# Transposes, operand casts and first-stage squares in another order, in a hybrid mLSTM and pooling encoder block

## The chip, the cores and the metric

The kernel runs on one core of a Trainium2 chip, as one launch. The metric is the device time of that launch in microseconds. The core's engines are TensorE (PE, matrix products), VectorE (DVE), ScalarE (ACT), GpSimd (POOL) and SyncE (SP, which here issues nearly all DMAs). Each engine runs its own instructions in program order and waits at semaphores for the others.

## The reference

One encoder layer on x of 2048 tokens by 1024 channels, in float32:

```
h   = rmsnorm(x) modulated by (shift, scale) of c
y   = mixer(h)            # mLSTM on half the channels, pooling on the other half
x   = x + gate * (y @ w_out)
h   = rmsnorm(x) modulated by (shift, scale) of c
x   = x + gate * (relu(h @ w_ff1)**2 @ w_ff2)
out = rmsnorm(x) * g_final
```

The mixer projects h to q, k, v, output gates, scan gates and u; runs a two-directional, chunkwise mLSTM scan over 4 heads; multiplies its normed result by sigmoid(o); and takes centred multi-scale means of u for the rest. The six modulation vectors are silu(c) times a 1024 x 6144 matrix, plus a bias.

## The kernel before

Float32 products are made of three products of parts: a *high* part (a cast to fp32r, on ACT) and a *low* part (the difference, on DVE), as high x high, high x low and low x high.

**The first stage** (0 to 140 us) norms four blocks of 512 tokens and makes v and the gates. For block 0, four loads of x (tiles `xt0` to `xt3`) are squared and summed on ACT (`stats`, L173), POOL makes the reciprocal roots, DVE makes diagonal matrices of them (`dg0`). Then for each of eight channel groups k, DVE makes two modulation sums (`mod_sum`, L117), PE transposes and scales x by the diagonal (`norm_first`, L214, into `xT`), ACT writes the modulated tile (`hf`, L207) and its high part (`Hh`, L208), and DVE the low part (`Hl`, L209). `vg_weights` splits the projection's weights (ACT L228, DVE L229), `vg_mm` does the projection of a 128-token tile. Blocks 1 to 3 (`later_block`) load x in rows (`xs4` and on, three buffers) for the squares `jk4` and on, and transposed (`xk`) for the data; their row statistics reach all partitions through PE (`rms_rows`, L202, `rb`). A scheduler orders this part and the stages up to about 648 us (other projections, the scan), except where `keep_in_program_order` holds an instruction in its place among its engine's instructions.

**The last stage** (from about 648 us) has a hand-written order. Its work is 72 *quads*: 8 of the set Out (y @ w_out, names `o00` to `o13`), 32 of First (h @ w_ff1, `f...`) and 32 of Second (`g...`). A quad handles 256 rows as a 2 x 2 block product in seven products instead of eight (operands 0 to 6: blocks or sums of blocks). A product is 12 matmuls of 128x512 on PE (`product`, L841). `step(t)` emits one step; quad n starts at step 7n, and with d = t - 7n its products stand at d = 0, 2, ... 12, so that from step 6 on each step has one product, taken in turns from two quads. In a step come, in this order: the product and its `post` (DVE add to `acc`, L945, or an ACT copy); for each quad near by its loads, sigmoid (L1004, `SIGM`) and gate (L1010, `GATE`), residual loads, `low_of` (DVE, L779), `sums_of` (DVE, `SUMS`: at d = 0 the two sums `s1`, `s2`, L864 and L865, of which operand 2 is the second), `high_of` (ACT, L776); then pieces of jobs that prepare sums of w_ff2 or h on DVE; then what earlier steps put off. Operand i's high part is made four steps and its low part three steps ahead of its product. There are four buffers for each.

An Out quad's rows, when done, are squared and summed (L953) at d = 13, scaled in place by ACT (`scaled`, L1033, twice) at d = 14, and turned at d = 15 to 18 (`turn`): each turn takes one PSUM bank `t` of two, transposes four 128 x 128 blocks into it (PE, L1043) and copies them with modulation to `hf` (ACT, L1045, in two halves); `put` stores that (L1051), and for the first four quads `sums` makes differences of it that are stored too (L1064). The `ob`, `hf` and job tiles share a pool of five buffers. Out's weights are the parts `ob_0` to `ob_6`, First's `hb`, split as they arrive (ACT L776, DVE L779, 128x1024 each).

## Time and profile before

| | us |
|---|---|
| median of 3 runs | 2110.2 |
| lowest, highest | 2106.39, 2110.89 |
| profiled execution, its own time | 2113.36 |
| its span, first to last instruction | 2111.6 |
| PE busy | 2006.0 |
| DVE busy | 1358.1 |
| ACT busy | 915.9 |

The profiled execution is one of the kernel's executions; its rows are compared with its own 2113.36 us, which is 3.2 us above the median. The stages by time: first stage 0 to 140 us, other projections to 262, scan to 648, Out to about 910, then First and Second to the end. The mean granted clock of TensorE over the span was 0.989 of full speed.

### The profile page before, as it was taken

Reading aid. Unit: us, or ns where it says so; the run is one execution under the profiler, and the core shown is the slowest. Engines: PE = TensorE matmul, PEld = TensorE weight load, DVE = VectorE, ACT = ScalarE, POOL = GpSimd, SP = SyncE. Lnnn points to the kernel's source line nnn. Section 1 sums busy time; section 2 is a strip of 40 time slices with the busy share of each in tenths; the row PEclk is TensorE's granted clock in tenths of the full one; section 3 lists DMA queues with packets and bytes.
Section 4 is the critical chain, followed back from the end, with each engine's and each line's share of the span. In section 5 each row is a group of like instructions: output and inputs, shape, how many; then the busy total and the mean of one; then the engine's idle time right before and its main releaser. Section 6 shows DMA issues by size and latency. Waiting matters only on the chain.

```text
span 2111.6 us, 27742 instructions
## 1 busy us (share of the span) xinstructions
PE 2006.0 (95%) x9591; PEld 1668.3 (79%) x9591; DVE 1358.1 (64%) x2456; ACT 915.9 (43%) x1704; POOL 131.8 (6%) x353
## 2 busy tenths in 40 slices
PE   7999999989999887799999999999999999999998
PEld 6897777878887666578888888888888888888887
DVE  6538646666627555545565766665876867767876
ACT  4631123323326555655555755555522423323432
POOL 1100012212210000100000000000000000000011
PEclk9999999999999999999999999999999999999999
DMA  8736867886548566656666766666887757657554
GB/s 325 231 105 213 274 196 225 253 252 210 177 150 261 175 211 224 198 160 187 197 214 221 232 224 225 208 213 196 289 278 236 264 170 216 245 174 249 202 162 137
DMA packets 298574, 452.87 MB, mean 214 GB/s; under 512 B 23569, under 2 KB 163137, under 8 KB 298306
## 3 DMA queue, kind: packets, MB, share of 16 engines
q1 hardware_dynamic: 228546, 413.35, 60.2%
q10 hardware_dynamic: 69888, 37.76, 5.8%
q8 instruction: 75, 1.23, 0.2%
q14 instruction: 65, 0.53, 0.1%
HBM read 290.40 MB, written 160.62 MB: 214 GB/s over the span
## 4 chain that ended last, share of the span: by engine, by line
PE 81%; DMA 7%; ACT 4%; DVE 4%; issue 2%; SPq 1%; POOL 1%; POOLq 0%; DVEq 0%; ACTq 0%
PE c L404 4%; PE c L405 4%; PE c L403 4%; DMA ua<-uad 2%; DMA ada<-in_w_ada 1%; DMA wotd<-os 1%; DMA vraw<-in_w_v 1%; PE o01x L841 1%; PE g313x L841 1%; PE g312x L841 1%; PE g311x L841 1%; PE g310x L841 1%; PE g303x L841 1%; PE g302x L841 1%; PE g301x L841 1%
## 5 line engine op out<-in xcount | busy, mean ns | idle before, releaser
L403 PE MATMUL c<-Hh,wh 128*128 128x512 f32 x512 | 211.5, 413 | 0.4 <-ACT wh L394 0.4
L404 PE MATMUL c<-Hl,wh 128*128 128x512 f32 x512 | 204.3, 399 | 0.0
L405 PE MATMUL c<-Hh,wl 128*128 128x512 f32 x512 | 203.5, 397 | 0.5 <-DVE wl L395 0.5
L405 PEld LDWEIGHTS c<-Hh,wl 128*128 128x128 f32 x512 | 97.0, 189 | 20.5 <-DVE wl L395 1.0
L403 PEld LDWEIGHTS c<-Hh,wh 128*128 128x128 f32 x512 | 97.2, 190 | 18.3 <-ACT wh L394 1.0
L404 PEld LDWEIGHTS c<-Hl,wh 128*128 128x128 f32 x512 | 97.4, 190 | 16.9 <-issue 0.7
L580 ACT ACTIVATE ua<-ua,vcol 128x128 f32<-128x128 f32 x64 | 25.6, 400 | 104.2 <-POOL ua L576 104.2
L117 DVE SCALAR_TENSOR_TENSOR ada<-ada,c_bc 128x1024 f32<-128x1024 f32 x48 | 58.0, 1220 | 19.1 <-DMA ada<-in_w_ada 19.0
L957 POOL TENSOR_TENSOR g300ss<-g300ss 128x1 f32<-128x1 f32 x2 | 0.9, 452 | 1087.6 <-ACT g300j L953 1087.6
L779 DVE TENSOR_TENSOR wb<-rwb,wb 128x1024 fp32r<-128x1024 f32 x56 | 68.2, 1218 | 0.4 <-ACT wb L776 0.3
L776 ACT CAST wb<-rwb 128x1024 fp32r<-128x1024 f32 x56 | 58.8, 1050 | 11.6 <-DMA rwb<-twd 11.6
L621 ACT ACTIVATE jk<-hm 128x128 bf16<-128x128 f32 x64 | 19.7, 308 | 81.3 <-DVE hm L619 80.7
L585 DVE TENSOR_TENSOR ua<-ua,q 128x256 f32<-128x256 f32 x64 | 26.5, 426 | 35.7 <-DMA ua<-uad 27.4
L576 POOL TENSOR_SCALAR_AFFINE_SELECT ua<-ua 128x128 f32<-128x128 f32 x64 | 24.5, 383 | 271.0 <-DMA ua<-uad 124.7
L624 DVE TENSOR_TENSOR hm<-hm,hss 128x256 f32<-128x256 f32 x32 | 14.8, 462 | 37.4 <-POOL hss L129 37.4
L779 DVE TENSOR_TENSOR ob<-rob,ob 128x1024 fp32r<-128x1024 f32 x14 | 17.0, 1223 | 33.6 <-ACT ob L776 33.3
L255 PE MATMUL vgp<-vgh,Hh 128*128 128x272 f32 x128 | 38.4, 301 | 0.0
L584 DVE TENSOR_TENSOR ua<-ua,S 128x256 f32<-128x256 f32 x64 | 26.5, 414 | 18.2 <-PE S L583 17.4
L256 PE MATMUL v2p<-v2h,Hh 128*128 128x256 f32 x128 | 37.0, 291 | 1.0 <-ACT v2h L236 1.0
L257 PE MATMUL vgp<-vgl,Hh 128*128 128x272 f32 x128 | 37.8, 296 | 0.0
L259 PE MATMUL vgp<-vgh,Hl 128*128 128x272 f32 x128 | 37.4, 294 | 0.0
L258 PE MATMUL v2p<-v2l,Hh 128*128 128x256 f32 x128 | 37.2, 292 | 0.0
(4048 smaller groups left out, 6081.0 us busy)
## 6 DMA issues: line engine op xcount, KB each, us to landing
rwb<-twd SPq DMA_DIRECT2D x56, 512.0 KB, 5.8
ada<-in_w_ada SPq DMA_DIRECT2D x48, 512.0 KB, 5.1
ua<-uad SPq DMA_DIRECT2D x64, 256.0 KB, 3.9
j<-in_w SPq DMA_DIRECT2D x32, 512.0 KB, 5.5
twd<-t SPq DMA_DIRECT2D x64, 256.0 KB, 3.1
twd<-j SPq DMA_DIRECT2D x48, 256.0 KB, 2.7
wr<-in_w_col SPq DMA_DIRECT2D x16, 512.0 KB, 5.2
q<-qkd SPq DMA_DIRECT2D x32, 256.0 KB, 3.6
```

The source lines that it names most:

```text
L117: ve.scalar_tensor_tensor(w, w, 1.0, c_bc, ALU.mult, ALU.mult, accum_out=mod[:, j:j + 1])
L255: pe.matmul(pa[:, :VG], hh, vgh[k], start=st, stop=False)
L256: pe.matmul(pb[:, :256], hh, v2h[k], start=st, stop=False)
L257: pe.matmul(pa[:, :VG], hh, vgl[k], start=False, stop=False)
L258: pe.matmul(pb[:, :256], hh, v2l[k], start=False, stop=False)
L259: pe.matmul(pa[:, :VG], hl, vgh[k], start=False, stop=en)
L403: pe.matmul(ps, hh[:, k], Hh[b][:, k], start=k == 0, stop=False)
L404: pe.matmul(ps, hh[:, k], Hl[b][:, k], start=False, stop=False)
L405: pe.matmul(ps, hl[:, k], Hh[b][:, k], start=False, stop=k == KT - 1)
L776: sc.copy(dst, src)
L779: ve.tensor_tensor(dst, src, asf(hi), ALU.subtract)
L841: pe.matmul(ps, a[:, k], b[:, k], start=start and k == 0 and n == 0, stop=k == 3 and n == 2, skip_group_check=not start)
```

## The change

There are four edits. In `turn`, the four transposes of a bank are issued first and the two copies behind them. Operand 2's high part is made at d = 1 instead of 0, its low part at d = 2 instead of 1 (all 72 quads). In the lead quad (`o00`), the second half's sigmoid and gate come one step earlier (-2 and -1). In the first stage, the small loads `bada` and `gmix` are issued ahead of the four loads of x, the first `vg_weights` stands behind the first `norm_first`, and the squares of block 1 (`jk4` to `jk7`) keep their place in the program, which is behind all of block 0.

```diff
--- before.py
+++ after.py
@@ -134,12 +134,12 @@
 
 
         ts = []
+        bada = small("bada", b_ada, 48)
+        gmix = small("gmix", g_mix, KT)
         for i in range(4):
             t = pv.tile([P, D], F32, tag="xt", name=f"xt{i}", bufs=4)
             dma(t, x[i * P:(i + 1) * P, :])
             ts.append(t)
-        bada = small("bada", b_ada, 48)
-        gmix = small("gmix", g_mix, KT)
         ada = []
         for k in range(0, KT, 2):
             w = big.tile([P, 4, D], F32, tag="big", name=f"ada_{k}")
@@ -171,7 +171,7 @@
             ss = rstd2[:, i:i + 1]
             junk = evt(f"jk{i}").bitcast(BF16)
             ins = sc.activation(junk[:, :D], t, AF.Square, accum_out=ss)
-            if i == 0:
+            if i < 8:
                 tc.keep_in_program_order(ins)
             rstd_of(ss, ss, D)
             return ss
@@ -274,7 +274,6 @@
         for j in range(4):
             ve.tensor_scalar(dg0[:, j], ident, stats(j, ts[j]), None, ALU.mult)
         h_tiles(0)
-        vg_weights(0)
         for k in range(KT):
             mod_sum(8 + k, ada[2 * k])
             mod_sum(k, ada[2 * k + 1])
@@ -282,6 +281,8 @@
             ve.scalar_tensor_tensor(s1[:, k:k + 1], mod[:, 8 + k:9 + k], bsc[:, k:k + 1], gmix[:, k:k + 1],
                                     ALU.add, ALU.mult)
             norm_first(k)
+            if k == 0:
+                vg_weights(0)
             if k % 2 and k < KT - 1:
                 vg_weights(k // 2 + 1)
             if k in (1, 3):
@@ -736,7 +737,10 @@
 
 
 
+
     SUMS = {0: 2, 3: 4, 5: 5}
+    HIGHS = {2 * i - (3 if i == 2 else 4): i for i in range(7)}
+    LOWS = {2 * i - (2 if i == 2 else 3): i for i in range(7)}
     with ExitStack() as fs:
         def room(name, bufs=1, **kw):
             return fs.enter_context(tc.tile_pool(name=name, bufs=bufs, **kw))
@@ -972,8 +976,8 @@
 
                 self.lead = s == j == 0
                 if self.lead:
-                    self.SIGM = {-6: 0, -1: 1}
-                    self.GATE = {-5: 0, 0: 1}
+                    self.SIGM = {-6: 0, -2: 1}
+                    self.GATE = {-5: 0, -1: 1}
                     self.EARLY = {3: (1, 1), 4: (0, 0), 5: (0, 1), 9: (1, 0)}
 
             def post(self, i, ps, slot):
@@ -1038,10 +1042,12 @@
                 hf = self.hf[m] = j4(f"{self.name}hf{m}")
                 for a in range(2):
                     k = 2 * m + a
-                    c = slice(256 * a, 256 * a + 256)
                     for h in range(2):
                         pe.transpose(pt[:, 256 * a + P * h:256 * a + P * h + P],
                                      self.acc[h, k // 4][:, k % 4 * P:k % 4 * P + P], ident)
+                for a in range(2):
+                    k = 2 * m + a
+                    c = slice(256 * a, 256 * a + 256)
                     sc.activation(hf[:, c], pt[:, c], AF.Identity, bias=mod[:, 24 + k:25 + k],
                                   scale=s2[:, k:k + 1])
 
@@ -1165,12 +1171,12 @@
                         (f if callable(f) else getattr(q, f))(when[d])
                 if d in q.EARLY:
                     q.residual(*q.EARLY[d])
-                if (d + 3) % 2 == 0 and 0 <= (d + 3) // 2 < NP:
-                    q.low_of((d + 3) // 2)
+                if d in LOWS:
+                    q.low_of(LOWS[d])
                 if d in SUMS:
                     q.sums_of(SUMS[d])
-                if (d + 4) % 2 == 0 and 0 <= (d + 4) // 2 < NP:
-                    q.high_of((d + 4) // 2)
+                if d in HIGHS:
+                    q.high_of(HIGHS[d])
             if t in jobs:
                 f, *args = jobs[t]
                 active.append(f(*args))
```

Lines behind the edits move: L776 becomes L780, L841 becomes L845, L1033 becomes L1037, L1043 becomes L1046, L1045 becomes L1051.

On PE, the first turn of the third quad (`o02`; `o02t` is the bank, `o02acc` the rows), with the engines that each row waits for. Before:

```order
L841 MATMUL o03x<-ob_6807,o034h 128x512 x2
L841 MATMUL o03x<-ob_6807,o034l 128x512
L1043 MATMUL o02t_7625<-ident,o02acc_7083 128x128 [waits PE_49,Activation_49]
L1043 MATMUL o02t_7625<-ident,o02acc_7417 128x128 [waits Activation_49]
L1043 MATMUL o02t_7625<-ident,o02acc_7083 128x128 [waits Activation_49]
L1043 MATMUL o02t_7625<-ident,o02acc_7417 128x128
L841 MATMUL o10y<-ob_6764,o101h 128x512 x2
```

After:

```order
L845 MATMUL o03x<-ob_6808,o034h 128x512 x2
L845 MATMUL o03x<-ob_6808,o034l 128x512
L1046 MATMUL o02t_7623<-ident,o02acc_7083 128x128 [waits PE_49,Activation_49]
L1046 MATMUL o02t_7623<-ident,o02acc_7415 128x128 [waits Activation_49]
L1046 MATMUL o02t_7623<-ident,o02acc_7083 128x128
L1046 MATMUL o02t_7623<-ident,o02acc_7415 128x128
L845 MATMUL o10y<-ob_6764,o101h 128x512 x2
```

The rows stand in the same order; the third transpose's wait for ACT is gone.

On ACT, the same place, from the cast of operand 5 of the fourth quad (`o035h`) to the second turn's copies (`o102h` is operand 2 of the fifth quad). Before:

```order
L776 CAST o035h_7557<-o03s2_7360 128x512
L953 ACTIVATE o02j10_7568,o02ss1_7433<-o02acc10_7417 128x512
L776 CAST o102h_7593<-o10s2_7590 128x512
L1033 ACTIVATE o02acc10_7417<-o02acc10_7417,o02ss1_7433 128x512
L1033 ACTIVATE o02acc11_7219<-o02acc11_7219,o02ss1_7433 128x512
L776 CAST o036h_7618<-o03y1_7139 128x512
L1004 ACTIVATE o11ob0_7531<-o11ob0_7531 128x512
L1045 ACTIVATE o02hf0_7626<-o02t0_7625,mod_90,s2_92 128x256 x2
L776 CAST o103h_7651<-o10s1_7589 128x512
L1045 ACTIVATE o02hf1_7655<-o02t1_7654,mod_90,s2_92 128x256 x2
```

After:

```order
L780 CAST o035h_7557<-o03s2_7360 128x512
L957 ACTIVATE o02j10_7568,o02ss1_7433<-o02acc10_7415 128x512
L1037 ACTIVATE o02acc10_7415<-o02acc10_7415,o02ss1_7433 128x512
L1037 ACTIVATE o02acc11_7219<-o02acc11_7219,o02ss1_7433 128x512
L780 CAST o036h_7616<-o03y1_7137 128x512
L780 CAST o102h_7620<-o10s2_7590 128x512
L1008 ACTIVATE o11ob0_7531<-o11ob0_7531 128x512
L1051 ACTIVATE o02hf0_7624<-o02t0_7623,mod_90,s2_92 128x256 x2
L780 CAST o103h_7651<-o10s1_7589 128x512
L1051 ACTIVATE o02hf1_7655<-o02t1_7654,mod_90,s2_92 128x256 x2
```

`o102h` moves from ahead of the two scalings to behind them and behind `o036h`; the two copies of a turn stand as before.

On ACT in the first stage, from the end of the fourth channel group of block 0 on (`jk` is a square of block 1, `hf0_k` and `Hh0` block 0's tiles). Before:

```order
L173 ACTIVATE jk4_410,rstd2_94<-xs4_408 128x1024
L207 ACTIVATE hf0_4_360<-xT4_355,mod_90,s1_91 128x512
L208 CAST Hh0_277<-hf0_4_360 128x512
L207 ACTIVATE hf0_5_373<-xT5_368,mod_90,s1_91 128x512
L208 CAST Hh0_277<-hf0_5_373 128x512
L228 CAST vgh3_377<-vraw_217 128x544
L207 ACTIVATE hf0_6_390<-xT6_385,mod_90,s1_91 128x512
L208 CAST Hh0_277<-hf0_6_390 128x512
L173 ACTIVATE jk5_417,rstd2_94<-xs5_415 128x1024
L207 ACTIVATE hf0_7_403<-xT7_398,mod_90,s1_91 128x512
L173 ACTIVATE jk6_424,rstd2_94<-xs6_422 128x1024
L208 CAST Hh0_277<-hf0_7_403 128x512
```

After:

```order
L207 ACTIVATE hf0_4_360<-xT4_355,mod_90,s1_91 128x512
L208 CAST Hh0_277<-hf0_4_360 128x512
L207 ACTIVATE hf0_5_373<-xT5_368,mod_90,s1_91 128x512
L208 CAST Hh0_277<-hf0_5_373 128x512
L228 CAST vgh3_377<-vraw_217 128x544
L207 ACTIVATE hf0_6_390<-xT6_385,mod_90,s1_91 128x512
L208 CAST Hh0_277<-hf0_6_390 128x512
L207 ACTIVATE hf0_7_403<-xT7_398,mod_90,s1_91 128x512
L208 CAST Hh0_277<-hf0_7_403 128x512
L173 ACTIVATE jk4_410,rstd2_94<-xs4_408 128x1024
L173 ACTIVATE jk5_417,rstd2_94<-xs5_415 128x1024
L173 ACTIVATE jk6_424,rstd2_94<-xs6_422 128x1024
```

`jk4` to `jk6` (and `jk7` behind the last row shown) move from between block 0's tiles to behind the last of them. On SP, the load of `xs7` moves behind block 1's four `xk` loads; the rest of the last stage's order on PE and SP is unchanged.

## Rows read from the trace of the kernel before

**Rows 1.** The page, chain of work that ended last, shares of the span by engine.
```profile
PE 81%; DMA 7%; ACT 4%; DVE 4%; issue 2%; SPq 1%; POOL 1%; POOLq 0%; DVEq 0%; ACTq 0%
```

**Rows 2.** Busy time by stretch: length, PE, PEld, DVE, ACT, POOL (instructions), PE clock, DMA, GB/s.
```profile
658.20:909.88 251.68, 203.20 (x885) 159.73 (x886) 144.49 (x229) 142.33 (x269) 20.69 (x48) 0.96 0.65 203
...
1200.00:2111.00 911.00, 904.00 (x3989) 748.20 (x3987) 647.26 (x953) 376.45 (x628) 18.77 (x48) 1.00 0.66 218
```

**Rows 3.** PE's waits, 690 to 912 us: total us, times, longest; best and worst quad.
```profile
PE o12t L1043 <- ACT o12hf L1045: 7.9, 4, 2.4
...
PE o00t L1043 <- ACT o00hf L1045: 3.9, 4, 1.8
PE o12t L1043 <- ACT o12acc L1033: 1.4, 1, 1.4
...
PE o13t L1043 <- ACT o13acc L1033: 0.8, 1, 0.8
```

**Rows 4.** Timeline of PE, a steady turn: start, length, instruction, [idle before, releaser].
```profile
729.79 0.38 PE L1043 MATMUL o01t<-ident,o01acc 128*128 128x128 f32 x2
730.89 0.44 PE L1043 MATMUL o01t<-ident,o01acc 128*128 128x128 f32 x2 [0.72 <-ACT o01hf L1045]
731.09 0.71 PE L841 MATMUL o03x<-ob,o032h 128*128 128x512 f32 x2
...
733.95 0.38 PE L1043 MATMUL o01t<-ident,o01acc 128*128 128x128 f32 x2
```

**Rows 5.** Timeline of PE, second pair of transposes in quad o02's first turn.
```profile
749.83 0.44 PE L1043 MATMUL o02t<-ident,o02acc 128*128 128x128 f32 x2 [1.78 <-ACT o02hf L1045]
```

**Rows 6.** Timeline of ACT ahead of that turn.
```profile
746.43 0.62 ACT L776 CAST o102h<-o10s 128x512 fp32r<-128x512 f32 x1 [4.41 <-PE o03x L841]
746.96 1.33 ACT L1033 ACTIVATE o02acc<-o02acc,o02ss 128x512 f32<-128x512 f32 x2
```

**Rows 7.** Timeline of DVE ahead of that cast.
```profile
745.65 0.69 DVE L865 TENSOR_TENSOR o10s<-o10s,o10y 128x512 f32<-128x512 f32 x1
```

**Rows 8.** Timeline of PE, the starts of two plain products in the last stage.
```profile
1551.68 0.61 PE L841 MATMUL g002z<-wb,g0025h 128*128 128x512 f32 x2
...
1554.40 0.61 PE L841 MATMUL g003x<-wb,g0032h 128*128 128x512 f32 x2
```

**Rows 9.** Timeline of DVE there, the low of the quad ahead's last operand.
```profile
1553.05 0.68 DVE L779 TENSOR_TENSOR g0026l<-g002w,g0026h 128x512 fp32r<-128x512 f32 x1
```

**Rows 10.** Busy time by stretch, a middle quad and a late quad of Out.
```profile
789.93:817.13 27.20, 22.04 (x102) 17.27 (x101) 15.54 (x29) 14.32 (x29) 2.49 (x6) 1.00 0.76 235
...
875.52:905.03 29.51, 23.63 (x101) 18.41 (x101) 15.33 (x21) 19.78 (x34) 3.51 (x6) 0.94 0.48 152
```

**Rows 11.** Timeline of PE, the lead quad's third product and the next one.
```profile
658.20 1.22 PE L841 MATMUL o00x<-ob,o002h 128*128 128x512 f32 x2 [4.88 <-ACT o002h L776]
...
663.20 0.63 PE L841 MATMUL o00z<-ob,o003h 128*128 128x512 f32 x2
```

**Rows 12.** Timeline of ACT there: the lead quad's second sigmoid and third operand.
```profile
654.09 0.62 ACT L1004 ACTIVATE o00ob<-o00ob 128x512 f32<-128x512 f32 x1
...
657.53 0.62 ACT L776 CAST o002h<-o00s 128x512 fp32r<-128x512 f32 x1 [2.34 <-DVE o00s L865]
```

**Rows 13.** Timeline of DVE there: the second low of part ob_4.
```profile
654.22 1.23 DVE L779 TENSOR_TENSOR ob<-rob,ob 128x1024 fp32r<-128x1024 f32 x1 [0.17 <-ACT ob L776]
```

**Rows 14.** Timeline of ACT in the first stage: the square of xs4.
```profile
37.03 1.06 ACT L173 ACTIVATE jk<-xs 128x1024 bf16<-128x1024 f32 x1 [5.54 <-DMA xs<-in_x]
```

**Rows 15.** Timeline of PE in the first stage, block 0's scaled transposes.
```profile
38.89 1.44 PE L214 MATMUL xT<-dg,xt 128*128 128x128 f32 x5 [5.30 <-ACT hf L207]
```

**Rows 16.** Busy time by stretch, right after that wait.
```profile
40.00:45.00 5.00, 5.00 (x25) 5.00 (x25) 5.00 (x12) 2.71 (x4) 0.00 (x0) 0.50 0.40 164
```

**Rows 17.** Timeline of DVE in the first stage, the low of block 0's fifth part.
```profile
39.52 0.69 DVE L209 TENSOR_TENSOR Hl<-hf,Hh 128x512 fp32r<-128x512 f32 x1 [3.92 <-ACT Hh L208]
```

**Rows 18.** PE's waits from 0 to 140 us, those for the statistics of blocks 1 to 3.
```profile
PE rb L202 <- DVE dg L190: 4.6, 3, 2.1
```

## The prediction

> **What bounds the kernel now.** I read the chain of waits first, then the busy time by stage, then PE's waits in the one stage that stands out, then single instructions there. The chain is 81% PE [rows 1]: only PE time, or a wait of PE, can be won. By stage [rows 2], from 1200 us to the end PE is busy 904.00 of 911.00 us, so nothing is to be had there but something can be lost. In the Out stage, 658.20 to 909.88 us, PE is busy 203.20 of 251.68 us: 48.5 us idle at a mean granted clock of 0.96, with neither ACT (142.33) nor DVE (144.49) full. PE's waits tell where [rows 3]: eight quads have four turns each, and in each quad the transposes wait four times for the copy `hf`, 3.9 us a quad in the best one and 7.9 in the worst (the eight sum to 39.2 us); once in each quad the first transposes also wait for `acc`, the scaling on ACT, 0.8 to 1.4 us (9.4 us in all). 39.2 + 9.4 = 48.6 is the whole idle time.
>
> A steady turn [rows 4]: first pair of transposes at 729.79, then a wait of 0.72 us for ACT's copy of that first pair, second pair at 730.89, product at 731.09, next turn at 733.95. Two transposes take 0.20 us with nothing in between (730.89 to 731.09); so the turn took 1.30 us, where four transposes need 0.40. In a quad's first turn the wait for the copy is 1.78 us [rows 5], because ACT reaches the copy late. Why it is late stands in [rows 6, 7]: on ACT `o102h` starts at 746.43, and only then the two scalings (746.96, 1.33 us); the profile names a product as what `o102h` waited for, but the sum it reads (`o10s`, L865) ran on DVE from 745.65 to 746.34, which fits its start to 0.1 us. So the third operand's cast holds the scaling, the scaling holds the first transposes, and the casts behind it hold the first copy.
>
> **The change, part by part.** *Turns.* With four transposes first and the copies behind, the third transpose has no wait. A turn is then 4 x 0.10 = 0.40 us, plus 0.14 us by which the product behind a turn is longer (2.86 from 731.09 to 733.95, against 2.72 between the starts of two plain ones [rows 8]): 0.54. The copies start 0.2 us later on ACT, which nothing on PE needs before the bank's next turn but one; that costs nothing while ACT has room, and 0.2 us a turn if it has none.
>
> *Third operand a step later.* The cast now stands behind the two scalings and `o036h`. Scaling then needs only the quad's row statistics, which do not depend on that sum, so it leaves the path: the 9.4 us of `acc` waits and the surplus of the first `hf` waits go. What comes late next is the third operand itself. Its low part is now made one product after its old place: after a product, DVE does the post add, the low of operand 6 and then this low, 3 x 0.68 = 2.0 us [rows 9]. The next product but one needs it with its third matmul, 2.72 + 2/12 x 2.72 = 3.17 us after the same end: 1.1 us spare. Where a job's sums are on DVE too, `g0026l` starts at 1553.05 [rows 9], so this low would end 2 x 0.68 later, at 1554.4, and is needed 0.45 us behind 1554.40 [rows 8]: 0.4 us spare. I take 0 us for all 72 quads; the bounds are 0 and, in a few quads with both a job and a new weight part on DVE (one more 0.68 in the way), 0.3 us.
>
> *The Out stage summed.* From 658.20 to 909.88 lie 63 products and 32 turns: 63 x 2.72 + 32 x 0.54 = 171.4 + 17.3 = 188.7 us against 251.7, 63.0 us less. That holds 48.5 of idle time and 14.5 of PE time that was longer than 2.72 a product: short stops stretch the matmuls behind them, and after the long ones the granted clock was lower (0.94 over the quad at 875.52 [rows 10]; the product at 658.20 took 5.0 us to 663.20, its first pair 1.22 us, the next product's 0.63 [rows 11]). Per quad this is 7 x 2.72 + 4 x 0.54 = 21.2 us instead of 27.2 [rows 10].
>
> *The lead quad.* PE waits 4.88 us for `o002h` [rows 11]. On ACT [rows 12] the sigmoid at 654.09 comes behind two casts of `ob_4`, which wait for their DMA; DVE then needs gate, sum and sum, and `o002h` runs at 657.53. Now sigmoid, gate and sums stand before those casts. But `o002h` still queues behind the casts and the copy L986: the copy takes the sigmoid's slot at 654.1, and if it is as long as that (0.6) `o002h` ends at 655.3. On DVE its low stands behind `ob_4`'s second low, which starts at 654.22 and ends at 655.45 [rows 13], and an add: 656.0 to 656.7, a 1 us wait inside the product. Effective start 656.3 instead of 658.20: 1.9 us. `o001h` now stands behind that sigmoid and a copy, up to 1.2 us later, under the product ahead of its own: 0, with 1.2 us lost as the bound. Out: 63.0 + 1.9 = 64.9.
>
> *What remains in Out.* In the last quads ACT is busy 19.78 us in 29.51 [rows 10] and would have 21.2; transposes or products will wait for it here and there. 1 to 2 us in each of the last three quads, up to 0.5 in each of the others: 6 us taken (bounds 0, and 18, 6 us for each of the three, as if the whole difference of their PE period, 27.2 to 21.2, stayed). Out: 59 us.
>
> *First stage.* ACT's square of `xs4` stands ahead of `hf0_4` and waits 5.54 us for its load [rows 14]; PE waits 5.30 us behind it [rows 15], and then runs 5 us at a granted clock of 0.50, the lower of the two levels (1.2 GHz), after the stop [rows 16]. With the squares behind block 0, `hf0_4` goes as soon as its scale is ready. DVE, which waited 3.92 us to 39.52 for what comes of it [rows 17], then goes on at 35.6: 3.9 us. The clock loss is 5 x 0.5 = 2.5 us. Against it, block 1's squares now run together behind `Hh0_7`, and the fourth one's load waits for the first square's buffer; PE's waits for these statistics were 4.6 us in three blocks [rows 18] and may grow or shrink, since the same change puts PE's `rb` matmuls behind more projection work. Bounds: nothing (the late squares take it all back) and 5.3 + 2.5 + 4.6 = 12. I take 7, the two measured parts 3.9 + 2.5 and half a us. The stages between are PE's own and pass it on.
>
> *`bada` and `gmix` ahead of `x`.* Two SP issues, 0.95 us; the first squares come that much later, the modulation's first sum that much earlier. 0, with 1.5 us lost as the bound. On small transfers, the Trainium skill ("DMA: Bandwidth & Descriptors", section "Why small descriptors are slow (HBM only)") speaks against it, with 27% overhead for 256-byte pieces; worked out from that page for the 28 KB here it is an estimate of 0.1 us, below what the sum takes. No row of this case shows these two loads ahead of `x`.
>
> **Sum.** 59 + 7 = 66 us from the profiled execution's 2113.4: 2047. That execution was 3.2 us above the median of 2110.2, so on the median 2044.
>
> **Rivals.** (1) *Transfers become the bound in Out.* In a middle quad the DMA engines are busy 0.76 of 27.20 us [rows 10], 20.7 us, and the new period is 21.2: 98%. Loads of `y` and stores of `hf` share few buffers, so full queues would hold the gate or the copy. For it: that share. Against: only the four quads of the first half store the extra differences, and loads are issued nine steps ahead. If no more than 85% can be had, such a quad takes 24.3 us: 3.1 us x 4 = 12 lost, 2056. The Trainium skill (the same page, "Where 436 GB/s comes from") gives 435 GB/s at most; by that page a quad's 6.4 MB are an estimate of 14.7 us, and this rival would be void. The trace does not agree: 235 GB/s at a share of 0.76 [rows 10] are 309 GB/s while busy, and I go by that row. (2) *The first turn keeps its wait*: if the scaling waits for something else than the cast, 9.4 + 8 x 1.1 = 18 us stay: 2062. With no gain in the first stage added to either, 2067 to 2069. (3) *The change does not do what it says in the turns*, the copies being needed before the fourth transpose: then only the third operand, the lead quad and the first stage help, about 20 us: 2090. (4) *Slower: the third operand's low comes too late on DVE.* It decides from its spare time of 0.4 to 1.1 us; to outweigh 66 us over the 64 quads behind Out, each must wait more than 1.03 us, so the low must come 1.4 to 2.1 us later than worked out in every quad. At 1.3 us a quad: 83 us lost, 2127. DVE, busy 647.26 of 911.00 us [rows 2], speaks against it.
>
> **How the numbers follow.** Forecast (gain of 54 to 82, 2028 to 2056): 0.70. Rivals 1 and 2, or no gain in the first stage on top of some residue, 2056 to 2068: 0.16; worse mixtures of these to 2085: 0.06. Rival 3: 0.03. Rival 4: 0.03, and 0.02 that some of it cancels the gain. Range 2028 to 2068. A measurement of this kernel tells 0.2% (4.2 us) from no change: faster 0.95, same 0.02, slower 0.03.
>
> **What would show it.** Right: no wait of a transpose for `hf`, none or nearly none for `acc`; a quad period near 21.2 us in the middle of Out; Out's 63 products and 32 turns in 188 to 206 us; `xT` of block 0 without a wait of 5 us; plain products still 2.72 us apart from 1200 us on. Wrong: PE waiting for lows of operand 2 in the First or Second quads; PE waiting in Out for casts that wait on loads, with the DMA share near 1; projection matmuls of blocks 1 to 3 waiting longer for their statistics than 4.6 us.

## The result and the profile after

The changed kernel takes 2054.86 us (median of 4 runs, 2052.05 to 2058.01) against 2110.51 for the kernel before (4 runs): a ratio of 0.9741, 95% interval 0.9722 to 0.9760, or 55.7 us. The time lies in the stated range (2028 to 2068), 11 us above the forecast of 2044. The profiled execution took 2054.10 us, 59.3 less than the profiled one of before; the steps below are compared between these two.

The page of the profile after, busy time, and the chain that ended last (it answers to [rows 1]):

```profile
PE 1991.4 (97%) x9591; PEld 1659.4 (81%) x9591; DVE 1356.0 (66%) x2456; ACT 917.9 (45%) x1704; POOL 132.0 (6%) x353
...
PE 74%; DMA 7%; DVE 4%; ACT 1%; issue 1%; SPq 1%; POOL 1%; POOLq 0%; DVEq 0%; ACTq 0%
```

PE is busy 14.6 us less than before (2006.0) with the same 9591 instructions. Most of that is the granted clock: in the trace of before, PE is busy for 35.2 us in stretches at 0.50, the lower of the two levels (1.2 GHz), and after for 12.6 us; at half speed the difference is worth 11.3 us.

Busy time by stretch, after, with the columns of [rows 2]. The first stretch answers to the Out stage there, from the effective start of the lead quad's third product to the same product of the First set as before; the second to the end of the kernel:

```profile
649.06:850.42 201.36, 192.36 (x884) 157.06 (x884) 142.45 (x227) 139.18 (x266) 23.01 (x48) 0.97 0.81 254
...
1143.40:2050.00 906.60, 901.26 (x3977) 746.18 (x3975) 645.26 (x952) 378.15 (x624) 18.70 (x48) 1.00 0.66 217
```

Out fell from 251.68 to 201.36 us; its idle PE time from 48.5 to 9.0. Behind Out nothing moved: the first product of quad `f010` starts 59.34 us earlier than before (893.94 against 953.28), and the last matmul of the kernel again 59.34 us earlier.

PE's waits in Out after (as [rows 3]):

```profile
PE o13t L1046 <- ACT o13acc L1037: 3.2, 1, 3.2
PE o12t L1046 <- ACT o12acc L1037: 2.8, 1, 2.8
PE o01t L1046 <- ACT o01acc L1037: 0.5, 1, 0.5
PE o02t L1046 <- ACT o02acc L1037: 0.4, 1, 0.4
PE o03t L1046 <- ACT o03acc L1037: 0.4, 1, 0.4
PE o10t L1046 <- ACT o10acc L1037: 0.2, 1, 0.2
```

All 32 waits for `hf` are gone. What is left of the turns' waits are those for the scaling, 7.5 us in sum, 6.0 of it in the last two quads. In the second of these waits, and 1.2 us behind the end of the first (811.65), the granted clock falls to the lower level, for 6.8 and 3.4 us (busy time by stretch, columns of [rows 2]):

```profile
812.87:816.29 3.42, 3.42 (x10) 2.58 (x9) 0.00 (x0) 2.28 (x5) 0.00 (x0) 0.50 0.95 323
836.77:843.59 6.82, 5.98 (x16) 4.72 (x17) 1.08 (x1) 3.63 (x7) 0.03 (x1) 0.50 0.14 40
```

PE is busy for 9.4 us there, which costs about 4.7 us.

Timeline of PE, a turn of quad o02 after (it answers to [rows 4]):

```profile
726.77 0.39 PE L845 MATMUL o10y<-ob,o101l 128*128 128x512 f32 x1
727.00 0.60 PE L1046 MATMUL o02t<-ident,o02acc 128*128 128x128 f32 x4
727.36 0.71 PE L845 MATMUL o03z<-ob,o035h 128*128 128x512 f32 x2
...
730.20 0.60 PE L1046 MATMUL o02t<-ident,o02acc 128*128 128x128 f32 x4
```

Four transposes stand in one row and take 0.36 us to the next product; from turn to turn 3.20 us, where it was 4.16.

But the first turn of most quads still waits. Timeline of ACT around it, quad o02 (it answers to [rows 6, 7]):

```profile
723.08 1.33 ACT L1037 ACTIVATE o02acc<-o02acc,o02ss 128x512 f32<-128x512 f32 x2 [4.10 <-DMA xad<-o02acc]
724.33 0.60 ACT L780 CAST o036h<-o03y 128x512 fp32r<-128x512 f32 x1
724.83 0.61 ACT L780 CAST o102h<-o10s 128x512 fp32r<-128x512 f32 x1
```

And of SP, which issues the DMAs:

```profile
717.05 2.74 SPq L1070 DMA_DIRECT2D thd<-o01T  x4
719.88 0.42 SPq L1186 DMA_DIRECT2D xad<-o02acc  x1
```

`o102h` is behind the scaling, as the change wants it. The scaling now waits 4.10 us for something else: it overwrites `o02acc` in place, and the store of the unscaled row to `xad`, which reads `o02acc`, must be through. SP issued that store only at 719.88, behind four stores of the last quad's sums.

### The profile page after: what moved, and what is told of

It reads as the page before. It is cut to its first block, busy times and chain, and to the rows that moved or that the text cites. A ratio compares the mean times of both kernels' runs of the same rounds, so it can differ in the third digit from the quotient of the medians.

```text
span 2052.2 us, 27784 instructions
## 1 busy us (share of the span) xinstructions
PE 1991.4 (97%) x9591; PEld 1659.4 (81%) x9591; DVE 1356.0 (66%) x2456; ACT 917.9 (45%) x1704; POOL 132.0 (6%) x353
## 4 chain that ended last, share of the span: by engine, by line
PE 74%; DMA 7%; DVE 4%; ACT 1%; issue 1%; SPq 1%; POOL 1%; POOLq 0%; DVEq 0%; ACTq 0%
PE c L406 3%; PE c L405 3%; PE c L404 3%; DMA ua<-uad 2%; DMA ada<-in_w_ada 1%; DMA os<-in_w_o 1%; PE g313x L845 1%; PE g312x L845 1%; PE g311x L845 1%; PE g310x L845 1%; PE g303x L845 1%; PE g302x L845 1%; PE g301x L845 1%; PE g300x L845 1%; PE g213x L845 1%
## 5 line engine op out<-in xcount | busy, mean ns | idle before, releaser
L581 ACT ACTIVATE ua<-ua,vcol 128x128 f32<-128x128 f32 x64 | 25.7, 401 | 106.8 <-POOL ua L577 106.8
L780 ACT CAST wb<-rwb 128x1024 fp32r<-128x1024 f32 x56 | 58.7, 1050 | 24.9 <-DMA rwb<-twd 24.8
L625 DVE TENSOR_TENSOR hm<-hm,hss 128x256 f32<-128x256 f32 x32 | 14.6, 457 | 39.0 <-POOL hss L129 39.0
L440 ACT COPY u<-c 128x512 f32<-128x512 f32 x16 | 9.4, 586 | 62.6 <-PE c L406 62.6
L585 DVE TENSOR_TENSOR ua<-ua,S 128x256 f32<-128x256 f32 x64 | 26.5, 414 | 14.6 <-PE S L584 14.2
```

The costliest lines, as they stand in the source:

```text
L585: ve.tensor_tensor(W, W, S[:, 0:P].unsqueeze(1).broadcast_to([P, 2, P]), ALU.mult)
L780: sc.copy(dst, src)
```

## Experiments: the parts alone

Each of the first four kernels is the kernel before with some of the change's edits. All medians of these four are compared with 2110.75 us, the kernel before on the same chip (19 runs).

**Turns alone.** Of the change only this:

```diff
                 for a in range(2):
                     k = 2 * m + a
-                    c = slice(256 * a, 256 * a + 256)
                     for h in range(2):
                         pe.transpose(...)
+                for a in range(2):
+                    k = 2 * m + a
+                    c = slice(256 * a, 256 * a + 256)
                     sc.activation(hf[:, c], pt[:, c], ...)
```

> Only the order inside a turn is changed: four transposes, then two copies. Theory (the wait for the copy is the turns' own, the wait for the scaling is the third operand's): the 39.2 us of waits for hf go, the 9.4 us for acc stay or grow a little, and part of the 14.5 us of stretched matmuls goes: 42 to 50 us less than before, about 2064. Rival (the transposes then wait for the scaling for longer, since ACT is late in every first turn): acc waits of 2 us and more a quad, 30 to 38 us less, about 2076.

Measured: 2063.35 us, ratio 0.9772 (0.9755 to 0.9788), 47.4 us less. PE's waits there:

```profile
PE o13t L1042 <- ACT o13acc L1033: 3.1, 1, 3.1
PE o12t L1042 <- ACT o12acc L1033: 2.3, 1, 2.3
PE o03t L1042 <- ACT o03acc L1033: 1.2, 1, 1.2
```

Five more quads wait 1.2 us each as o03 does. So the copy's wait was the order of the turn, and the waits for the scaling stayed at 1.2 us, as the first theory had it; in o12 and o13 they grew from 1.4 and 0.8 to 2.3 and 3.1. That PE now comes there earlier fits this, but was not tried by itself.

**Third operand alone.**

```diff
+    HIGHS = {2 * i - (3 if i == 2 else 4): i for i in range(7)}
+    LOWS = {2 * i - (2 if i == 2 else 3): i for i in range(7)}
...
-                if (d + 3) % 2 == 0 and 0 <= (d + 3) // 2 < NP:
-                    q.low_of((d + 3) // 2)
+                if d in LOWS:
+                    q.low_of(LOWS[d])
```

(and the same for `high_of` with `HIGHS`)

> Only operand 2's high and low part are a step later. Theory: the acc waits (9.4 us) go, and each first turn's wait for hf falls from 1.8 to the 0.7 of the other turns (8 x 1.1 us): 12 to 18 us less than before, about 2095; from 1200 us on products stay 2.72 us apart. Rival (the cast was not what held the scaling): no change, 2108 to 2112. Second rival (the later low is too late on DVE): slower than before, with PE waiting for lows of operand 2.

Measured: 2106.69 us (10 runs, 2099.79 to 2110.39), ratio 0.9977 (0.9965 to 0.9990): 4.1 us less, a third of what was expected. Its profiled execution (2102.33) is the second fastest of the ten. There six of eight waits for `acc` are gone, but the wait for the first copy hardly fell. Four rows of PE's waits there:

```profile
PE o02t L1045 <- ACT o02hf L1047: 3.9, 4, 1.7
...
PE o00t L1045 <- ACT o00hf L1047: 3.6, 4, 1.5
PE o12t L1045 <- ACT o12acc L1035: 1.3, 1, 1.3
PE o13t L1045 <- ACT o13acc L1035: 0.8, 1, 0.8
```

The longest wait for a copy is 1.5 to 1.8 us in the first five quads, where 0.7 was expected: the casts between the scaling and the first copy still stand there, `o102h` itself among them. The mechanism for `acc` is confirmed, the second term was wrong. And ACT already waits for something new here, which costs PE nothing in this quad yet (the first turns of o02 and o03 are still 25.7 us apart):

```profile
ACT o02acc L1035 <- DMA xad<-o02acc: 2.9, 1, 2.9
```

**Both.**

> Turns and third operand together, first stage and lead quad as before. Theory (the rest of the change is worth 5.8 us in the first stage and 3.3 in the lead quad): 45 to 50 us less than before, about 2064. If the two parts only overlap, it is no faster than the better of the two alone; if each takes its own wait, it is 10 to 16 us faster than the turns alone.

Measured: 2057.98 us, ratio 0.9748 (0.9728 to 0.9769), 52.8 us less: 5.4 us better than the turns alone, half of the least that was expected (the intervals of the two overlap), and again 2.4 and 2.8 us of waiting for `acc` in o12 and o13.

**The first stage alone** (small loads first, `vg_weights(0)` behind `norm_first(0)`, squares of block 1 kept in program order; the edits as in the change):

> Only the first stage's edits (small loads first, weights split later, squares behind block 0). Theory: 5 to 6.5 us less than before, all of it there by the last projection of v and kept to the end, about 2104.5. Rival (the gain is lost again in the scheduled stages behind): under 2 us.

Measured: 2107.11 us (10 runs), ratio 0.9980 (0.9970 to 0.9989), 3.6 us less, between theory and rival. In its profiled execution the last projection of v is 6.5 us earlier than in that of before, but 4.5 us of that are lost again in Out, with the same waits as before. What differs there is the granted clock; busy time by stretch of about one quad, in that execution:

```profile
740.00:767.00 27.00, 21.84 (x100) 17.13 (x99) 15.34 (x29) 14.32 (x29) 2.49 (x6) 1.00 0.72 219
767.00:797.00 30.00, 24.91 (x103) 19.30 (x101) 15.85 (x29) 14.42 (x29) 2.48 (x6) 0.89 0.65 195
797.00:825.00 28.00, 22.85 (x99) 17.96 (x98) 12.11 (x20) 14.32 (x29) 1.92 (x6) 0.94 0.68 217
```

Per matmul that is 0.218 us at a clock of 1.00 and 0.242 at 0.89, so the second stretch has 2.4 us more PE time for its 103 matmuls. That execution (2111.49) is the slowest of this kernel's ten, so its loss is not the rule; the median counts.

**The change without one part.** Three single executions, to be read by places and not by totals.

Without the small loads first:

```diff
-        bada = small("bada", b_ada, 48)
-        gmix = small("gmix", g_mix, KT)
         for i in range(4):
             ...
+        bada = small("bada", b_ada, 48)
+        gmix = small("gmix", g_mix, KT)
```

> The whole change without the small loads ahead of x. Theory (the two issues cost the start 0.7 us): the first transposed matmul is at 11.7 us instead of 12.4, the last v projection up to 1 us earlier, the total the same within its interval. Rival (the modulation sums wait for bada): the start moves, but the first scale of block 0 does not, and nothing is gained behind it.

The first transposed matmul is at 11.76 us against 12.38: these loads ahead of x cost 0.6 us there, and this is clear of the spread (11.6 to 11.8 in all five executions without them, 12.3 to 13.5 in all nine with them). The last v projection is 0.9 us earlier (132.92), which is inside the spread of that place. The total (2051.26) is within the spread of the change's runs.

With the squares where they were (`if i == 0:` in `stats`):

> The whole change, with the squares of the second block where the scheduler put them before. Theory (the first stage's gain is theirs): PE waits some 5 us again behind the square of xs4, and the last v projection is back at 136.5 to 140.5 us instead of 133.8. Rival (the later split of the weights makes the gain): it stays at 133 to 135.

Timeline of PE in the first stage there (2057.05 in all):

```profile
39.92 2.08 PE L214 MATMUL xT<-dg,xt 128*128 128x128 f32 x8 [5.47 <-ACT hf L207]
```

The wait of 5.30 us [rows 15] is back as 5.47, and the last v projection is at 140.47 us. The first stage's gain is the squares': with the small loads first and the weights split later, but without them, nothing is won.

Without the earlier sigmoid and gate (`SIGM` -1 and `GATE` 0 again):

> The whole change without the earlier sigmoid and gate of the lead quad. Theory (they are worth the difference between 4.9 and 1.5 us of waiting at that quad's third product, and a shorter time at the lower clock): the gap from its second to its third product is 6.9 to 7.8 us instead of 3.7, and what follows runs as in the whole change.

Timeline of PE at the lead quad's third product there (2059.47 in all):

```profile
657.84 1.22 PE L844 MATMUL o00x<-ob,o002h 128*128 128x512 f32 x2 [5.72 <-ACT o002h L779]
```

The gap from the lead quad's second to its third product is 8.60 us (649.24 to 657.84) instead of 3.70, a little more than expected. The seven executions with both this edit and the later third operand show 3.70 to 4.75.

## Experiments: what holds the last quads

The waits in o12 and o13, and the scaling's wait for the store, were left. Each kernel here is the whole change with one more edit. They ran on several chips, on which the kernel before took 2110.47 to 2112.71 us; a difference between the medians of two of them is uncertain by about as much, 2 us.

**Squares first.** Work that a step has put off is done in the order in which it was put off; here the square of a finished row is taken ahead.

```diff
-            for f, args in later.pop(t, ()):
+            for f, args in sorted(later.pop(t, ()), key=lambda e: getattr(e[0], "__name__", "") != "square"):
```

> The whole change, and of the work that a step has put off the sum of squares of a finished row is done first, ahead of the casts of the next set's weight parts and of the turns' copies (other work of a step keeps its order). Theory (the 2.8 and 3.2 us for which PE waits for acc in quads o12 and o13 come from ACT, where the square stands behind those casts, so that POOL's root comes late and ACT then waits for it): both waits fall to under 1.5 us, the granted clock in these quads stays nearer 1.00, and the time falls by 4 to 7 us against the whole change, to about 2049. Rival (ACT is simply full there): the waits stay near 6 us in sum, 2052 to 2057.

Measured: 2050.99 us, ratio to before 0.9714 (0.9698 to 0.9731). By the medians that is 3.9 us less than the change, but the two intervals overlap, so the gain is not clear of the spread. Nor did it come as expected: o12 still waits 2.5 us and o13 2.2. In this execution the granted clock in the last quads stayed at 1.00, where the change's fell for 3.4 and 6.8 us; but it also stayed there in the run without the earlier sigmoid, whose squares stand as in the change. ACT's waits name the other cause:

```profile
ACT o02acc L1036 <- DMA xad<-o02acc: 4.0, 1, 4.0
...
ACT o12acc L1036 <- DMA xad<-o12acc: 3.7, 2, 1.9
```

**No scaling in place.** DVE makes a diagonal of the reciprocal roots, the turns multiply by it, nothing overwrites the row.

```diff
             def scaled(self, h):
-                for a in (self.acc[h, 0], self.acc[h, 1]):
-                    sc.mul(a, a, self.ss[h][:, 0:1])
+                self.dg[h] = pdg.tile([P, P], F32, tag="dg", name=f"{self.name}dg{h}")
+                ve.tensor_scalar(self.dg[h], ident, self.ss[h][:, 0:1], None, ALU.mult)
...
-                        pe.transpose(pt[...], self.acc[h, k // 4][...], ident)
+                        pe.matmul(pt[...], self.acc[h, k // 4][...], self.dg[h],
+                                  start=True, stop=True)
```

> The whole change, but Out's rows are no longer scaled in place by ACT: DVE makes a diagonal matrix of the reciprocal roots, and the turns multiply by that instead of transposing with the identity (as the first stage does). Theory (after the change ACT waits 2 to 4 us in each quad for the store of the unscaled row, which reads what the scaling overwrites, and PE's waits for acc in o01 to o10 and in o12 come of that): ACT has no wait for that store, PE's waits for acc or the diagonal fall from 7.4 us in sum to under 3 us, and the time falls by 3 to 7 us against the whole change, to about 2050. Rival (the waits in o12 and o13 are a full ACT or a late root): o12 and o13 still wait 4 us or more in sum for the diagonal, 2053 to 2057. Third: if a product with the diagonal takes longer on PE than a transpose, 128 of them show it in the time of a turn.

Measured: 2056.88 us, ratio 0.9748 (0.9733 to 0.9762), no gain. Yet the waits fell as the theory has it, to 1.1 us in o12 and 0.5 in o13, with none in the six quads ahead of them; so a late root alone does not explain them. The third possibility took the gain; timeline of PE, a turn:

```profile
730.39 1.05 PE L1046 MATMUL o02t<-o02dg,o02acc 128*128 128x128 f32 x8
731.20 0.71 PE L845 MATMUL o03z<-ob,o035h 128*128 128x512 f32 x2
```

Four products with the diagonal run as eight matmuls and take 0.81 us to the next product, where four transposes took 0.36: 32 turns x 0.45 = 14.4 us more. With squares first on top:

> The diagonal of the run before it, and the squares of finished rows first among the work put off. Theory (store and late root are two causes): o12 and o13 wait under 1 us in sum, 6 to 10 us less than the whole change, about 2047. If the diagonal alone already takes all waits, the two runs agree within 1 us.

2055.39 us, ratio 0.9743 (0.9726 to 0.9760): o12 and o13 wait 0.5 us each, and the total stays, for the same reason.

**Stores first.** Scaling in place again; in the list of work put off, the stores and the squares of finished rows come first, so that SP issues the store ahead of the loads of weight parts, which wait for their buffers, and of the stores of `hf` and of its sums.

```diff
-            for f, args in later.pop(t, ()):
+            for f, args in sorted(later.pop(t, ()), key=lambda e: not (
+                    e[0] is dma or getattr(e[0], "__name__", "") == "square")):
```

> The whole change with scaling in place; of the work put off in a step, the stores of finished rows and their squares come first, so that on SP the store no longer stands behind the loads of the next set's weight parts, which wait for their buffers. Theory (the store is late because it is issued late): ACT's waits for it fall from about 4 to 2 us in o01 to o10, little in PE's time there, and o12's wait falls by 1 us or more: 4 to 7 us less than the whole change, as with squares first or a little more. Rival (the store is late because transfers are slow, a DMA share of 0.85 to 0.96 in these quads): the waits stay as they are.

Measured: 2040.90 us (2038.86 to 2043.78), ratio to before 0.9675 (0.9656 to 0.9694): 70.8 us less than before, 14 less than the change and 10 less than squares first. It beats both kernels. Out, from the lead quad's third product to the first of `f010`, takes 232.6 us in the profiled execution, against 245.6 in that of the change and 240.2 with squares first: 13.0 and 7.6 us of the gains are there, and the rest lies ahead of that, where the kernels are the same. (The edit also takes stores in Second ahead; from `f010` on, both the change and this version take 1150.7 to 1150.8 us.) PE's waits for `acc`, all that there are:

```profile
PE o13t L1045 <- ACT o13acc L1036: 1.0, 1, 1.0
```

ACT's waits for the store, the two that are left:

```profile
ACT o02acc L1036 <- DMA xad<-o02acc: 2.1, 1, 2.1
ACT o10acc L1036 <- DMA xad<-o10acc: 1.8, 1, 1.8
```

Around the same place as above, the timeline of SP:

```profile
712.15 0.49 SPq L1186 DMA_DIRECT2D xad<-o02acc  x1
712.73 1.04 SPq L1056 DMA_DIRECT2D h2d<-o01hf  x2
713.83 2.36 SPq L1069 DMA_DIRECT2D thd<-o01T  x4
```

and of ACT:

```profile
716.49 1.34 ACT L1036 ACTIVATE o02acc<-o02acc,o02ss 128x512 f32<-128x512 f32 x2 [2.06 <-DMA xad<-o02acc]
```

The store goes ahead of 3.4 us of other issues, and the scaling is through at 717.8, 0.9 us ahead of the turn's first transpose (718.66). In the change it was through at 724.4, 1.2 us behind the turn's first transpose (723.21). From o02 to o13 quads are 20.96 us apart. Transfers were not short: in this kernel's busiest stretch the DMA share was 0.99 and PE waited for nothing:

```profile
788.00:809.00 21.00, 21.00 (x102) 17.38 (x101) 18.61 (x24) 19.91 (x36) 4.23 (x6) 1.00 0.99 311
```

**Stores first, without the later third operand.**

> The version with stores and squares of finished rows first, without the later third operand (all other parts of the change kept). Theory (the cast of the third operand held the scaling as worked out, and its gain was hidden because the store then held it): PE waits about 1.2 us for acc in each of seven or eight quads again, 8 to 10 us in sum instead of 1.0, and the time is 8 to 12 us above the 2040.9 us of the version with it, about 2050. Rival (with the store early, the cast no longer matters, since the scaling is reached in time either way): the waits stay near 1 us in sum, 2039 to 2043.

Measured: 2053.01 us, ratio 0.9719 (0.9695 to 0.9742), 12.1 us above the version with it. Two rows of PE's waits:

```profile
PE o12t L1043 <- ACT o12acc L1034: 1.3, 1, 1.3
PE o03t L1043 <- ACT o03acc L1034: 1.2, 1, 1.2
```

Seven quads wait 1.2 or 1.3 us for `acc` again and o13 1.0: 9.5 us in sum. So by the medians the later third operand is worth 12 us where the store is in time, and 5.4 where it is not (turns alone against both). In the profiled executions the waits for `acc` fall by 8.6 us (9.6 to 1.0) and by 5.9 (12.6 to 6.7), and Out by 11.0 (243.6 to 232.6) and by 3.2 (246.6 to 243.5). So the late store and square hold back some 3 us of waiting. The rest of the difference is in good part the clock: with both, it fell to the lower level for 6.8 us right at the wait in o13, and neither with the turns alone nor in these two versions did it fall in the last quads. Busy time by stretch, both:

```profile
838.20:845.00 6.80, 6.06 (x17) 4.80 (x18) 0.99 (x2) 3.68 (x7) 0.00 (x0) 0.50 0.14 39
```

## Why the prediction was right, and where it was not

The time came out inside the range, and most of the gain (47.4 of 55.7 us) comes from the mechanism that was forecast for the turns. By the medians the gain is near the lower end of the forecast one (54 to 82). Term by term, by the two profiled executions:

| term | forecast | measured |
|---|---|---|
| Out, steady part | 57.0 | 251.68 - 201.36 = 50.3 |
| lead quad | 1.9 | 3.3 |
| first stage | 7 | 5.8 |
| stages between, First, Second | 0 | 0 |
| sum | 66 | 59.3 |

**Turns: right.** No wait for `hf` is left, a turn has one row of four transposes, and turns alone gave 47.4 us. From turn to turn 3.20 us pass, 0.48 more than a product's 2.72, where 0.54 was forecast.

**Third operand: the wrong step is "scaling then needs only the quad's row statistics".** It also needs the store of the row that it overwrites. In the trace of before nothing waits for that store, because the cast held the scaling for longer than the store did; the step should have asked which other reader of `acc` is late when the cast is gone. This is the prediction's second rival, come true in part: the scaling does wait for something else, but PE's waits for `acc` are 7.5 us, 6.0 of them in two quads, and not 9.4 with another 8.8 for the first copies. The runs show it from three sides: ACT waits 2.9 us for `xad` with the third operand alone and 4 us in the change; making the store earlier takes PE's waits for `acc` from 6.1 us with squares first to 1.0, and 7.6 us off Out; and the third operand takes 8.6 us of these waits away then, 5.9 before. The term "the surplus of the first `hf` waits" did not come from this part either; the turns' order takes it.

**What remains in Out: 6 us forecast, 12.7 measured** (201.36 against the ideal 188.7). Of that 9.0 is idle PE time (7.5 for `acc`, 0.9 for the low of `o012`, the rest in small pieces) and 3.7 more busy time: the two stretches at the lower clock cost about 4.7, and the cheaper turns give 1.9 back. The sum had no term for the clock here. The place was right, the last quads, but the cause was put down to a full ACT; it was the store and the late square, for with both first, ACT is busy 19.91 of 21.00 us in such a stretch and PE waits for nothing. Of the two the store is the one that is shown, since squares first left 4.7 us of waiting in o12 and o13.

**Lead quad: 3.3 instead of 1.9, in part luck.** PE waits 0.81 us for `o002h` and 0.73 for its low (1 was forecast). As forecast, `o002h` stands behind two casts of `ob_4`; but these started 2.95 us behind the quad's first product (641.91), as their load landed, where before it was 4.02 (651.74 against 647.72). Timeline of ACT after:

```profile
644.86 1.05 ACT L780 CAST ob<-rob 128x1024 fp32r<-128x1024 f32 x1 [1.11 <-DMA rob<-wotd]
```

In the other six executions with both the earlier sigmoid and the later third operand they started 3.3 to 4.0 us behind it, and the lead quad gained 2.3 to 3.0 us against before. Timeline of PE after:

```profile
648.33 0.73 PE L845 MATMUL o00x<-ob,o002h 128*128 128x512 f32 x2 [0.81 <-ACT o002h L780]
649.79 0.50 PE L845 MATMUL o00x<-ob,o002l 128*128 128x512 f32 x1 [0.73 <-DVE o002l L783]
```

Here, with a shorter stop, the first pair took 0.73 us instead of 1.22 [rows 11], and the granted clock stayed at 1.00.

**First stage: mis-sized.** The pair of profiled executions shows 5.8 us, but the last v projection varies without the change (136.6 to 139.6 in the four executions whose first stage is as before) and with it (132.7 to 137.4 in eight): 138.0 and 134.6 on the mean, 3.4 us. The stage alone gave 3.6 by its median. With the change the spread is the granted clock again: 132.7 to 134.1 in the five executions where it stayed at 1.00 between 60 and 140 us, 135.8 in the two where it fell for 3.4 us near 95 us, and 137.4 in the one where it fell for 6.8 us, at a wait of PE for a block's statistics (stores first without the later third operand, busy time by stretch):

```profile
94.50:101.20 6.70, 5.88 (x27) 5.89 (x28) 5.34 (x10) 3.89 (x6) 0.65 (x3) 0.50 0.41 120
```

DVE's 3.9 us were there (the low of `hf0_4` starts at 36.58 instead of 39.52, and `hf0_2` had been 1.0 us later than before), and so was what the prediction set against them without taking any of it off: the fourth square comes last and waits for its load. Timeline of ACT after:

```profile
50.49 1.06 ACT L173 ACTIVATE jk<-xs 128x1024 bf16<-128x1024 f32 x1 [1.54 <-DMA xs<-in_x]
```

The diagonals of block 1 are complete at 52.9 us (53.9 before): block 1 goes on only 1 us earlier. PE's waits for such statistics did not grow, though: 3.5 us in sum instead of 4.6 [rows 18].

**The small loads** cost 0.6 us at the first matmul, inside the bound of 1.5; taken as 0.

**Rivals.** Transfers did not become the bound: the share rose, to 0.79 to 0.89 over the change's quads and to 0.98 over one of stores first, and no wait of PE in Out names a load. At a share of 0.99 the engines moved 311 GB/s, as the 309 worked out from [rows 10] had it. That one store held the scaling was a matter of where it stood in SP's order. The rival of a late low came true once outside the lead quad, 0.88 us in o01, more than the 0.3 us that was its bound for a quad; there Out's weight parts and the lead quad's extra adds are on DVE. A load has a part in it: DVE waited 1.33 us for a residual and then ran without a stop up to this low. Timelines of DVE and PE after:

```profile
660.50 0.69 DVE L949 TENSOR_TENSOR o01acc<-o01x,o01acc 128x512 f32<-128x512 f32 x1 [1.33 <-DMA o01acc<-in_x]
...
667.30 0.50 PE L845 MATMUL o01x<-ob,o012l 128*128 128x512 f32 x1 [0.88 <-DVE o012l L783]
```

Behind Out, no wait of PE is in the trace at all. One figure of the prediction was added up wrongly: the first rival without the first stage's gain is 2056 + 7 = 2063, not 2067; nothing else hangs on it.

## What to carry to other kernels

Where one engine writes a PSUM bank in several pieces and another reads it in pieces, write all pieces first: alternating put a round trip between every two pieces, here 0.7 to 2.4 us, 32 times, and matmuls behind such stops were longer too. When an instruction that overwrites a tile in place is freed from one wait, list every other reader of that tile, its store above all, and look at what stands ahead of that store in the queue that issues it. A gain that seems small for its mechanism may be hidden by the next wait, and by what the clock does behind that wait: the same edit took 3 us off Out with the store late and 11 us with it early.

## What the runs showed that was not expected

The granted clock differs between executions of one kernel, and most of their spread goes with it. With the first stage's edits alone and the same waits as before in Out, 100 matmuls took 21.84 us of PE time at 1.00, and 103 took 24.91 at 0.89. Ten runs of the third operand alone lay 10.6 us apart, from 2099.79 to 2110.39, and their mean granted clock goes with the time, from 0.992 in the fastest to 0.987 in the slowest; 0.005 of 2100 us is 10.5 us.

In the traces the falls to the lower level in Out stand at waits of PE, but not every wait brings one. In the last quads the change's clock fell for 10.2 us in sum; in its three versions without one part, with waits of 2.1 to 2.8 us there, it fell for 3.4, 3.4 and 0 us; in the two versions with the diagonal and the two with stores first, where these waits are 1.3 us or less, it did not fall. Why the same wait brings a fall in one execution and none in another was not tried and stays open.

Here a multiplication by a diagonal in fp32 costs PE more than twice a transpose of the same block: 0.81 against 0.36 us for four of 128x128, as eight matmuls instead of four.
